# Weight buffers, normalised input tiles and FFN activation tiles begin at eight different 16-byte offsets

## The chip, the core and the metric

The kernel runs on one core of one Trainium2 chip. The metric is the device time of one execution in microseconds (us); lower is better. Before the change the median of three runs is 1369.74 us.

## What is computed

The reference is a decoder trunk of two layers over 512 tokens with a model width of 1024, in float32. Layer 0 is a recurrent mixer (an RG-LRU beside an SSD), layer 1 is dilated attention with 16 heads, and each is followed by a SwiGLU feed-forward network (FFN) with 2816 hidden channels. Cut to its products:

```python
for layer in range(2):
    if layer == 0:
        proj = rmsnorm(x) @ w_in                        # 1024 -> 4624
        ...                                             # convolutions, scans, gates
        x = x + concat(lru_out, ssd_out) @ w_out        # 2048 -> 1024
    else:
        qkv = rmsnorm(x) @ w_qkv                        # 1024 -> 3072
        ...                                             # attention
        x = x + o @ w_out                               # 1024 -> 1024
    g, u = split(rmsnorm(x) @ w_gate_up)                # 1024 -> 2 * 2816
    x = x + (silu(g) * u) @ w_down                      # 2816 -> 1024
```

## The kernel before

Activations lie with channels on the partitions and the 512 tokens along the free axis, so a tile of 128 channels is 128 x 512 float32, 2048 bytes in each partition. A projection of 1024 channels has eight such input tiles.

**Split products.** TensorE multiplies in the format fp32r, which keeps fewer bits than float32. Every operand of a large product is therefore split in two: a high part (the value rounded to fp32r) and a low part (the rest). ScalarE (ACT) writes the high part by a cast, and VectorE (DVE), or GpSimd (POOL) for the attention weights, writes the low part by a subtraction; this is `split` (L82). One product of a weight tile with an input tile is then three matmuls, `mm3` (L104), in a fixed order: low weight with high input (L106), high weight with low input (L107), high with high (L108). Each streams the 512 token columns of the input tile (the moving operand) through 128 x 128 weights that were loaded before (the stationary operand). The load of a matmul's weights (PEld in the profile) runs while the matmul ahead of it streams. In the attention projections (L720 to L722) the roles are turned: the tokens of the input tile are the stationary operand and 512 columns of a weight tile move.

**Weights.** All large weights go through one list of specs in the order of use. `weight(i)` (L89) works two tiles ahead. For tile j it issues one DMA of 128 x 1024 floats into a buffer `wr`, and splits it into `wh` and `wl`. Each of the three has three buffers in turn, of 4096 bytes per partition.

**Inputs.** `Norm.feed` (L179) multiplies a residual tile by the gain of the norm and writes it as `xh` and `xl` into a numbered slot (`slot`, L167); there are twelve slots, and the outputs of the RG-LRU, of the SSD and of the attention heads use the same slots where they fit. The others lie in other pools (`oah`, `oal`, `obh`, `obl`). In the FFN (L645) the silu products are split into `ah` and `al`, twelve buffers of each. A part of 7 or 8 hidden tiles is made by gate and up projections from `xh` and `xl`, and then multiplied by the down weights from `ah` and `al`; there are three such parts in each FFN.

**Counts.** The large products are 5184 matmuls of 512 columns: 2112 gate and up (FFN), 1056 down (FFN), 864 input projections and 384 output projections of the recurrent layer, 576 of q, k and v, and 192 of the attention output.

**Order.** The order on each engine is that in which the code is traced, with waits on semaphores between engines.

**Where the buffers lie.** The program places a buffer at a multiple of 32 bytes in the partition. Taken modulo 512 bytes, every tile of a weight (stationary operand, L106 to L108) starts at byte 96. So do all the slots of `xh` and `xl`; `ah` and `al` start at 288, and `oah`, `oal`, `obh` and `obl` at 480. The small stationary tile `wdt` of L295 starts at 480. The displacement of the moving operand from the stationary one, modulo 512, is thus 0 in 3936 of the 5184 matmuls, 192 in the 1056 of the down projections, and 384 in 192 of the recurrent output projection.

Of the kernel before, what the change touches and what calls it, by code (L numbers as in the profile page):

```python
# [28 lines left out]

# [1 line left out]
_PV = {}  # L31
# [16 lines left out]

# [1 line left out]
_CS = {}  # L50
# [8 lines left out]
def trunk(ctx: ExitStack, tc: tile.TileContext, a):  # L59
# [10 lines left out]

    # ------------------------------------------------------------ weights
    specs = []
# [9 lines left out]
    def split(src, hi, lo, eng=V):  # L82
        S.copy(hi, src)  # L83
        eng.tensor_tensor(out=lo, in0=src, in1=hi.bitcast(F32), op=ALU.subtract)  # L84

    w_of = {}
    emitted = [0]

    def weight(i):  # L89
        while emitted[0] <= min(i + AHEAD, len(specs) - 1):  # L90
            j = emitted[0]
            src, n = specs[j]
            raw = wp.tile([P, WMAX], F32, tag="raw", bufs=NRAW, name=f"wr{j}")
            hi = wp.tile([P, WMAX], F32R, tag="whi", bufs=NSPL, name=f"wh{j}")
            lo = wp.tile([P, WMAX], F32R, tag="wlo", bufs=NSPL, name=f"wl{j}")
            step = n if j else n // 4
            for c in range(0, n, step):
                nc.sync.dma_start(out=raw[:, c:c + step], in_=src[:, c:c + step])
                split(raw[:, c:c + step], hi[:, c:c + step], lo[:, c:c + step], G if src.tensor.name in on_pool else V)
            w_of[j] = (hi, lo)  # L100
            emitted[0] += 1
        return w_of.pop(i, None)
# [6 lines left out]

    # weight order  # L110
    rec_order = [("p", m) for m in (32, 33, 34, 35)]
# [30 lines left out]

    # ------------------------------------------------------------ constants, input
    def load_x(k):
# [12 lines left out]
    def pc(name, i=0, n=1):  # L157
        o, _ = _PV[name]
        return pv[:, o + i:o + i + n]
# [5 lines left out]

    # ------------------------------------------------------------ norm pieces
    def slot(i, dtype):  # L167
        return [xp.tile([P, T], dtype, tag=f"x{z}{i}", name=f"x{z}{i}") for z in "hl"]

# [31 lines left out]
    def rsq_tok(acc, n, eps, tag):  # L201
        """[token, tile] of (sum over partitions of acc / n + eps) ** -0.5"""
        ps = pm.tile([P, T], F32, tag="pm", name="ps_ss")
        for j in range(NT):
            mm(ps[:, j:j + 1], lhsT=acc[:, j * P:(j + 1) * P], rhs=ones[:, 0:1], start=True, stop=True)
        v = sp.tile([P, NT], F32, tag="rv", name="rv")
        V.tensor_scalar(out=v, in0=ps[:, :NT], scalar1=1.0 / n, scalar2=eps, op0=ALU.mult, op1=ALU.add)
        r = sp.tile([P, NT], F32, tag=tag, name=tag)
        G.tensor_tensor(out=r, in0=v, in1=mhalf[:, :NT], op=ALU.pow)
        return r  # L210
# [8 lines left out]

    # work that is traced behind the products of the next projection, which run while its operands are made  # L220
    held = []
# [12 lines left out]

    # ============================================================ layer 0: mixers
    norm = Norm("rec_norm")
# [11 lines left out]
    with ExitStack() as rctx:  # L248
# [6 lines left out]
        rt2 = pctx.enter_context(tc.tile_pool(name="rt2", bufs=2))  # L255
        # dt: the high part of its weights in columns 0..15, the low part in columns 32..47
        wdt = rt2.tile([P, KD, P], F32R, name="wdt", bufs=1)
        G.memset(wdt.rearrange("p k c -> p (k c)").bitcast(mybir.dt.uint32), 0)
        split(wdt_raw, wdt[:, :, :H], wdt[:, :, 32:32 + H])

        # softplus(v) = max(v, 0) + log1p(exp(-|v|)); 1 + u is rounded, and the rest of u is put back
        def softplus(out, v, shape, tag):
# [14 lines left out]

        # --- depthwise causal convolution of a projected tile
        def conv(ps, wname, bname, j, out):
            xin = rp.tile([P, T], F32, tag="cin", name="cin", bufs=2)  # L280
            V.tensor_tensor(out=xin, in0=ps, in1=rb, op=ALU.mult)
            w = lambda t: pc(wname, j * 4 + t)  # noqa: E731
            V.tensor_scalar(out=out, in0=xin, scalar1=w(3), scalar2=pc(bname, j), op0=ALU.mult, op1=ALU.add)
            for t in range(3):
                s = 3 - t
                V.scalar_tensor_tensor(out=out[:, s:], in0=xin[:, :T - s], scalar=w(t), in1=out[:, s:], op0=ALU.mult, op1=ALU.add)

        # --- SSD inputs
        BC = []
# [9 lines left out]
        for j in range(4):  # L299
# [5 lines left out]
            BC.append(t)  # L305
        # --- dt
        dtT = rt2.tile([32 + H, T], F32, name="dtT", bufs=1)
# [14 lines left out]
        softplus(dt, dtv, [P, NH], "sd")  # L322
        # lru: c = -8 softplus(-lambda), halved for the tanh form of the gate
        nlam = rt2.tile([P, 8], F32, name="nlam", bufs=1)
# [65 lines left out]

        # gelu of the gate of tile j
        gg, hs = {}, {}
# [72 lines left out]

        # --- RG-LRU
        lru = {}
# [34 lines left out]

        # --- gated LRU output
        oa = []
# [76 lines left out]

        # --- SSD heads and their gate, with the LRU half of the output projection
        def zlate(j, zz):
# [59 lines left out]

    # ============================================================ feed-forward
    def ffn(norm, idx, after):  # L645
        gu, dn = idx
        with ExitStack() as fctx:
            fp = fctx.enter_context(tc.tile_pool(name="fp", bufs=1))
            pre = [project(gu[0], norm.hl)]
            norm.finish()  # L650
            pre.append(project(gu[KF], norm.hl))
            rb = bcast_tok(norm.rt, fp, "nrb")
            for part, (first, last) in enumerate(HID):
                act = []
                for m in range(first, last):
                    pg, pu = pre if m == 0 else [project(gu[i], norm.hl) for i in (m, m + KF)]
                    tg = fp.tile([P, T], F32, tag="tg", name="tg", bufs=3)
                    tu = fp.tile([P, T], F32, tag="tu", name="tu", bufs=3)
                    V.tensor_tensor(out=tg, in0=pg, in1=rb, op=ALU.mult)  # L659
                    S.activation(tg, tg, AF.Silu)  # L660
                    V.tensor_tensor(out=tu, in0=pu, in1=rb, op=ALU.mult)  # L661
                    V.tensor_tensor(out=tu, in0=tu, in1=tg, op=ALU.mult)
                    hi = fp.tile([P, T], F32R, tag="ah", name="ah", bufs=12)
                    lo = fp.tile([P, T], F32R, tag="al", name="al", bufs=12)
                    split(tu, hi, lo)
                    act.append((hi, lo))
                for m in range(8):
                    ps = project(dn[part, m], act)
                    V.tensor_tensor(out=x[m], in0=ps, in1=x[m], op=ALU.add)  # L669
                    if part == len(HID) - 1:  # L670
                        after(m)
# [3 lines left out]

    # ============================================================ layer 1: attention
    norm = norm2
    norm3 = Norm("ffn_norm1", (8, 9, 10, 11, 4, 5, 6, 7))
    with ExitStack() as actx:
# [6 lines left out]
        gains = []  # L686
        # rotary tables with the gains of the rotated dimensions in them
        tabs = {}
# [16 lines left out]
        def qkv_part(half, w):  # L705
            """projection of 512 columns for all tokens, as a list of steps"""
            pss = []
# [23 lines left out]
        def finish_qk(half, w, t, ps):  # L731
# [10 lines left out]
            V.tensor_tensor(out=q, in0=q, in1=rs.rearrange("p (h o) -> p h o", o=1).to_broadcast([P, 8, 64]), op=ALU.mult)  # L742
            tb = lambda nm: tabs[w, nm][:, t].rearrange("p (o e) -> p o e", o=1).to_broadcast([P, 8, 8])  # noqa: E731
            x1, x2 = q[:, :, 0:8], q[:, :, 8:16]
# [9 lines left out]
        def pair_T(pair):  # L754
            half, p = pair // 4, pair % 4
            for w in range(2):
# [3 lines left out]
                g = gains[w]  # L760
                # head 0 keeps its high part on partitions 0..63, head 1 on partitions 64..127
                hs_ = [ap_.tile([P, T], F32R, tag=f"hi{w}{e}", bufs=2, name="qk_hi") for e in range(2)]
# [19 lines left out]
        oT = []  # L782
        # score rows of token tile i (i + 1 key tiles) and the transposed key tile j (NT - j token tiles), in banks
        S_AT = {3: (0, 0), 0: (1, 0), 2: (1, P), 1: (2, 0)}
# [105 lines left out]

# [1 line left out]
def _tiles(w, kt):  # L892
    """[k, m] -> [m tile, partition of k, k tile, column]"""
    k, m = w.shape
    return w.reshape(kt, P, m // P, P).transpose(2, 1, 0, 3).reshape(m // P, P, kt * P)


def _chan(v):
    """channels -> [partition, tile]"""
    return v.reshape(-1, P).T  # L900
# [6 lines left out]
def _consts():  # L907
# [12 lines left out]
    ang = (np.arange(T, dtype=f)[:, None] * inv[None, :]).astype(f)  # L920
    tok = lambda v: v.reshape(NT, P, 8).transpose(1, 0, 2).reshape(P, NT * 8)  # noqa: E731
    rot = (i % 64) < 16
# [55 lines left out]
```

## Time and profile before

| what | value |
|---|---|
| median of 3 runs | 1369.74 us (1369.41 to 1369.77) |
| profiled execution, first to last instruction (its span) | 1367.8 us |
| profiled execution, time of its own beside the span | not listed; the median of the runs is 1.9 us above the span |
| TensorE busy with matmuls | 1346.5 us, 98% of the span |
| VectorE, ScalarE, GpSimd busy | 797.2, 573.4, 148.5 us |
| mean granted TensorE clock | 0.997 of full speed |

The busy time of TensorE is the union of its matmuls, which overlap: a matmul of 512 columns is recorded with about 390 ns from its start to its modelled end, while the next one starts some 230 ns after it. For the pace of the products the start times are to be compared, and not the durations.

### The profile page before, as it was taken

How to read it: one execution, taken by the hardware profiler on the slowest of the kernel's cores; microseconds unless marked ns; L12 is line 12 of the kernel's file. 1: busy time of each engine (PE TensorE's matmuls, PEld its weight loads, DVE VectorE, ACT ScalarE, POOL GpSimd, SP SyncE). 2: the span in 40 equal slices, each digit the busy share in tenths (PEclk: the TensorE clock that was granted, in tenths of full speed). 3: DMA queues.
4: the chain of work that ended last, by engine and by line, in shares of the span. 5: the costliest groups of instructions: out<-in, count | busy, mean ns of one | idle time of the engine just before them, and what ended most of it. 6: DMA issues, size and time to landing. Idle time of an engine off the chain costs nothing.

```text
span 1367.8 us, 15662 instructions
## 1 busy us (share of the span) xinstructions
PE 1346.5 (98%) x6058; PEld 1081.3 (79%) x6058; DVE 797.2 (58%) x1332; ACT 573.4 (42%) x842; POOL 148.5 (11%) x123
## 2 busy tenths in 40 slices
PE   7999989999999999999999999999999999999998
PEld 6877767888888888888888877777788888888887
DVE  6877799865454334434454777687664434443442
ACT  5743857433332223223333378567642222222321
POOL 0000000000000000000005744554300000000000
PEclk9999999999999999999999999999999999999999
DMA  6322222522233333333232221121033332233332
GB/s 235 109 92 78 93 78 82 165 93 93 92 93 98 103 92 92 92 102 100 85 100 92 77 78 32 62 77 47 18 106 95 105 93 93 91 94 108 93 93 77
DMA packets 38554, 126.50 MB, mean 92 GB/s; under 512 B 4288, under 2 KB 5056, under 8 KB 38352
## 3 DMA queue, kind: packets, MB, share of 16 engines
q1 hardware_dynamic: 38480, 125.51, 29.6%
q8 instruction: 47, 0.77, 0.2%
q14 instruction: 27, 0.22, 0.1%
HBM read 123.36 MB, written 2.13 MB: 92 GB/s over the span
## 4 chain that ended last, share of the span: by engine, by line
PE 87%; DVE 8%; ACT 2%; POOL 2%; issue 1%; DMA 0%; SPq 0%; POOLq 0%; DVEq 0%; ACTq 0%
PE ps_pr L106 24%; PE ps_pr L107 24%; PE ps_pr L108 24%; PE ps_s L803 2%; POOL qrs L741 1%; DVE q L742 1%; PE ps_s L804 1%; PE ps_qkv L721 1%; PE ps_qkv L720 1%; PE ps_qkv L722 1%; PE ps_pT L830 1%; PE ps_o L837 1%; PE ps_ao L106 1%; DVE q L750 1%; PE ps_ao L107 1%; PE ps_yd L543 1%
## 5 line engine op out<-in xcount | busy, mean ns | idle before, releaser
L83 ACT CAST wh<-wr 128x1024 fp32r<-128x1024 f32 (+2 forms) x223 | 228.0, 1023 | 632.7 <-PE ps_pr L108 398.6
L106 PE MATMUL ps_pr<-xh,wl 128*128 128x512 f32 x1056 | 416.9, 395 | 12.2 <-DVE wl L84 11.2
L107 PE MATMUL ps_pr<-xl,wh 128*128 128x512 f32 x1056 | 415.3, 393 | 0.9 <-DVE xl L183 0.9
L108 PE MATMUL ps_pr<-xh,wh 128*128 128x512 f32 x1056 | 414.1, 392 | 0.0
L84 DVE TENSOR_TENSOR wl<-wr,wh 128x1024 fp32r<-128x1024 f32 (+2 forms) x191 | 225.9, 1183 | 52.9 <-ACT wh L83 52.6
L106 PEld LDWEIGHTS ps_pr<-xh,wl 128*128 128x128 f32 x1056 | 199.8, 189 | 55.4 <-DVE wl L84 12.1
L107 PEld LDWEIGHTS ps_pr<-xl,wh 128*128 128x128 f32 x1056 | 199.7, 189 | 43.8 <-DVE xl L183 1.8
L108 PEld LDWEIGHTS ps_pr<-xh,wh 128*128 128x128 f32 x1056 | 199.6, 189 | 42.3 <-issue 0.7
L107 PE MATMUL ps_pr<-al,wh 128*128 128x512 f32 x352 | 138.8, 394 | 0.0
L106 PE MATMUL ps_pr<-ah,wl 128*128 128x512 f32 x352 | 138.8, 394 | 0.0
L108 PE MATMUL ps_pr<-ah,wh 128*128 128x512 f32 x352 | 138.8, 394 | 0.0
L84 POOL TENSOR_TENSOR wl<-wr,wh 128x1024 fp32r<-128x1024 f32 x32 | 78.2, 2448 | 398.7 <-ACT wh L83 398.5
L669 DVE TENSOR_TENSOR x<-ps_pr,x 128x512 f32<-128x512 f32 x48 | 33.2, 692 | 127.7 <-PE ps_pr L108 127.7
L661 DVE TENSOR_TENSOR tu<-ps_pr,nrb 128x512 f32<-128x512 f32 x44 | 30.4, 691 | 130.1 <-PE ps_pr L108 130.1
L659 DVE TENSOR_TENSOR tg<-ps_pr,nrb 128x512 f32<-128x512 f32 x44 | 30.4, 691 | 93.8 <-PE ps_pr L108 93.8
L108 PEld LDWEIGHTS ps_pr<-ah,wh 128*128 128x128 f32 x352 | 65.9, 187 | 16.3
L106 PEld LDWEIGHTS ps_pr<-ah,wl 128*128 128x128 f32 x352 | 65.9, 187 | 16.2
L107 PEld LDWEIGHTS ps_pr<-al,wh 128*128 128x128 f32 x352 | 65.9, 187 | 16.2
L720 PE MATMUL ps_qkv<-wh,xl 128*128 128x512 f32 x192 | 75.6, 394 | 0.5 <-ACT q L734 0.5
L721 PE MATMUL ps_qkv<-wl,xh 128*128 128x512 f32 x192 | 75.7, 394 | 0.0
L722 PE MATMUL ps_qkv<-wh,xh 128*128 128x512 f32 x192 | 75.6, 394 | 0.0
L720 PEld LDWEIGHTS ps_qkv<-wh,xl 128*128 128x128 f32 x192 | 36.1, 188 | 7.8 <-ACT q L734 1.0
(231 smaller groups left out, 1591.3 us busy)
## 6 DMA issues: line engine op xcount, KB each, us to landing
wr<-in_w_gu SPq DMA_DIRECT2D x88, 512.0 KB, 3.5
wr<-in_w_in SPq DMA_DIRECT2D x35, 512.0 KB, 3.6
wr<-in_w_dn SPq DMA_DIRECT2D x32, 448.0 KB, 3.3
wr<-in_w_qkv SPq DMA_DIRECT2D x24, 512.0 KB, 3.5
wr<-in_w_out SPq DMA_DIRECT2D x16, 512.0 KB, 3.5
wr<-in_w_dn SPq DMA_DIRECT2D x16, 512.0 KB, 3.5
x<-in_xT SPq DMA_DIRECT2D x16, 256.0 KB, 3.5
bcs<-csd SPq DMA_DIRECT2D x16, 256.0 KB, 4.1
```

The lines of the kernel that those rows point to most:

```text
L83: S.copy(hi, src)
L84: eng.tensor_tensor(out=lo, in0=src, in1=hi.bitcast(F32), op=ALU.subtract)
L106: mm(ps, lhsT=wl[ws], rhs=xh[xs], start=start, stop=False)
L107: mm(ps, lhsT=wh[ws], rhs=xl[xs], start=False, stop=False)
L108: mm(ps, lhsT=wh[ws], rhs=xh[xs], start=False, stop=stop)
L659: V.tensor_tensor(out=tg, in0=pg, in1=rb, op=ALU.mult)
L661: V.tensor_tensor(out=tu, in0=pu, in1=rb, op=ALU.mult)
L669: V.tensor_tensor(out=x[m], in0=ps, in1=x[m], op=ALU.add)
L720: mm(pss[t], lhsT=xl[:, ts_], rhs=wh[:, cols], start=(k == 0), stop=False)
L721: mm(pss[t], lhsT=xh[:, ts_], rhs=wl[:, cols], start=False, stop=False)
L722: mm(pss[t], lhsT=xh[:, ts_], rhs=wh[:, cols], start=False, stop=(k == KD - 1))
L803: mm(ps, lhsT=q[rows, qs], rhs=kl[rows, :n], start=True, stop=False)
```

## The change

A helper `shifted` allocates a tile with 32 more columns (128 bytes) than wanted and returns the wanted number of columns from an offset of 0, 4, ... or 28 floats, that is 0, 16, ... or 112 bytes. The index that picks the offset is the number of the weight for `wh`, that number divided by 8 for `wl`, the number of the slot for `xh` and of the slot plus 3 for `xl`, and the number of the hidden tile for `ah` and of the tile plus 3 for `al`. The DMA's buffer `wr`, `wdt`, and the tiles `oah`, `oal`, `obh` and `obl` are not shifted, but all that is allocated behind a longer buffer moves with it.

```diff
+    def shifted(pool, n, dtype, i, **kw):
+        o = 4 * (i % 8)
+        return pool.tile([P, n + 32], dtype, **kw)[:, o:o + n]
...
-            hi = wp.tile([P, WMAX], F32R, tag="whi", bufs=NSPL, name=f"wh{j}")
-            lo = wp.tile([P, WMAX], F32R, tag="wlo", bufs=NSPL, name=f"wl{j}")
+            hi = shifted(wp, WMAX, F32R, j, tag="whi", bufs=NSPL, name=f"wh{j}")
+            lo = shifted(wp, WMAX, F32R, j // 8, tag="wlo", bufs=NSPL, name=f"wl{j}")
...
     def slot(i, dtype):
-        return [xp.tile([P, T], dtype, tag=f"x{z}{i}", name=f"x{z}{i}") for z in "hl"]
+        return [shifted(xp, T, dtype, i + 3 * (z == "l"), tag=f"x{z}{i}", name=f"x{z}{i}") for z in "hl"]
...
-                    hi = fp.tile([P, T], F32R, tag="ah", name="ah", bufs=12)
-                    lo = fp.tile([P, T], F32R, tag="al", name="al", bufs=12)
+                    hi = shifted(fp, T, F32R, m, tag="ah", name="ah", bufs=12)
+                    lo = shifted(fp, T, F32R, m + 3, tag="al", name="al", bufs=12)
```

The rest of the difference is comments taken out. Every engine keeps its instructions, their order and their waits; only addresses differ. In the built program the displacement of the moving from the stationary operand takes all 32 multiples of 16 bytes modulo 512, each in 136 to 184 of the 5184 matmuls.

## Rows read from the trace of the kernel before

**Rows 1.** The page: busy time by engine, slices of TensorE and its clock.

```profile
PE 1346.5 (98%) x6058; PEld 1081.3 (79%) x6058; DVE 797.2 (58%) x1332; ACT 573.4 (42%) x842; POOL 148.5 (11%) x123
...
PE   7999989999999999999999999999999999999998
...
PEclk9999999999999999999999999999999999999999
```

**Rows 2.** The page: the chain that ended last, shares of the span by engine.

```profile
PE 87%; DVE 8%; ACT 2%; POOL 2%; issue 1%; DMA 0%; SPq 0%; POOLq 0%; DVEq 0%; ACTq 0%
```

**Rows 3.** Waits: who waited for whom, us, times, longest.

```profile
ACT wh L83 <- PE ps_pr L108: 398.6, 119, 8.9
...
PE ps_pr L106 <- DVE wl L84: 11.2, 3, 6.0
```

**Rows 4.** Timeline of TensorE, FFN gate and up: start, duration; first to last 176 intervals.

```profile
400.03 0.39 PE L108 MATMUL ps_pr<-xh,wh 128*128 128x512 f32 x1
400.26 0.39 PE L106 MATMUL ps_pr<-xh,wl 128*128 128x512 f32 x1
...
439.93 0.39 PE L107 MATMUL ps_pr<-xl,wh 128*128 128x512 f32 x1
```

**Rows 5.** Timeline of TensorE, FFN down; 111 intervals from the first to the last.

```profile
575.06 0.40 PE L106 MATMUL ps_pr<-ah,wl 128*128 128x512 f32 x1
575.29 0.39 PE L107 MATMUL ps_pr<-al,wh 128*128 128x512 f32 x1
...
600.96 0.40 PE L106 MATMUL ps_pr<-ah,wl 128*128 128x512 f32 x1
```

**Rows 6.** Busy time and counts in a gate-and-up and a down stretch: us, PE, PEld, DVE, ACT, POOL.

```profile
400.00:460.00 60.00, 60.00 (x265) 49.44 (x264) 27.10 (x32) 17.33 (x21) 0.00 (x0) 1.00 0.33 98
575.00:600.00 25.00, 25.00 (x108) 20.04 (x108) 8.92 (x10) 4.70 (x5) 0.00 (x0) 1.00 0.33 99
```

**Rows 7.** Timeline of TensorE, recurrent output projection, tiles ob; first to last 12 intervals.

```profile
331.22 0.39 PE L106 MATMUL ps_pr<-obh,wl 128*128 128x512 f32 x1
...
331.68 0.40 PE L108 MATMUL ps_pr<-obh,wh 128*128 128x512 f32 x1
331.92 0.39 PE L106 MATMUL ps_pr<-obh,wl 128*128 128x512 f32 x1
332.14 0.40 PE L107 MATMUL ps_pr<-obl,wh 128*128 128x512 f32 x1
332.38 0.39 PE L108 MATMUL ps_pr<-obh,wh 128*128 128x512 f32 x1
...
334.01 0.39 PE L106 MATMUL ps_pr<-xh,wl 128*128 128x512 f32 x1
```

**Rows 8.** The chain in order of time: start, us, what; two longer pieces.

```profile
16.56 3.72 PE ps_dt L295 x16
...
88.70 2.58 PE ps_st L432 x6
```

**Rows 9.** Timeline, start of the second FFN; from 1006.74 first 11, then 7 intervals.

```profile
1005.61 0.95 PE L205 MATMUL ps_ss<-cst,nacc 128*128 128x1 f32 x8
1006.42 0.48 PE L107 MATMUL ps_pr<-xl,wh 128*128 128x512 f32 x1
1006.74 0.39 PE L108 MATMUL ps_pr<-xh,wh 128*128 128x512 f32 x1
1006.97 0.40 PE L106 MATMUL ps_pr<-xh,wl 128*128 128x512 f32 x1
...
1009.27 0.39 PE L107 MATMUL ps_pr<-xl,wh 128*128 128x512 f32 x1
...
1010.86 0.39 PE L108 MATMUL ps_pr<-xh,wh 128*128 128x512 f32 x1
```

**Rows 10.** Groups by shape: convolution steps, and splits; busy us, mean ns, idle before.

```profile
L286 DVE SCALAR_TENSOR_TENSOR cv<-cin,pv,cv 128x509 f32<-128x509 f32 x12 | 8.9, 745 | 0.2
L286 DVE SCALAR_TENSOR_TENSOR cv<-cin,pv,cv 128x511 f32<-128x511 f32 x12 | 8.8, 744 | 0.1
...
L549 DVE SCALAR_TENSOR_TENSOR xs<-xs,pv,ps_yd 128x512 f32<-128x512 f32 x8 | 6.0, 746 | 6.1 <-PE ps_yd L543 6.1
```

**Rows 11.** The page: groups of the casts and subtractions of the weights.

```profile
L83 ACT CAST wh<-wr 128x1024 fp32r<-128x1024 f32 (+2 forms) x223 | 228.0, 1023 | 632.7 <-PE ps_pr L108 398.6
...
L84 DVE TENSOR_TENSOR wl<-wr,wh 128x1024 fp32r<-128x1024 f32 (+2 forms) x191 | 225.9, 1183 | 52.9 <-ACT wh L83 52.6
...
L84 POOL TENSOR_TENSOR wl<-wr,wh 128x1024 fp32r<-128x1024 f32 x32 | 78.2, 2448 | 398.7 <-ACT wh L83 398.5
```

## Prediction

> **What bounds the kernel now.** I read the page first. TensorE is busy in 98% of the span, in nearly all of its slices nine tenths or more, and its granted clock is full throughout [rows 1]. The chain that ended last runs through TensorE for 87% of the span; VectorE has 8%, ACT and POOL 2% each, DMA none [rows 2]. So the pace of the matmuls sets the time. The waits agree: the longest is ACT's, 398.6 us, for the matmul that frees a weight buffer, while the matmuls wait 11.2 us in all for their split weights [rows 3]. The weights are early, TensorE is late.
>
> Next comes the pace itself, read from start times. In the gate and up projections of the FFN the reader sees a start every 0.22 or 0.23 us: 39.90 us for 176 intervals, 226.7 ns each [rows 4]. In the down projections it is 25.90 us for 111 intervals, 233.3 ns [rows 5]. Both are matmuls of 512 columns with 128 x 128 weights, at the full clock of 2.4 GHz, without a gap: busy time equals the length of both stretches [rows 6]. At one column per cycle 512 columns take 213.3 ns. Each matmul so pays 13.4 or 20.0 ns beyond its columns, and the 5184 together some 80 us. The two stages don't differ in instruction, clock or waits. They differ in addresses: the moving operand lies 0 bytes (modulo 512) from the stationary one in gate and up, 192 bytes in down.
>
> Two more places show a dependence. Where `ob` moves, at displacement 384, starts alternate between some 0.23 and 0.24 us, 2.79 us for 12 intervals, 232.5 ns [rows 7]. The 16 products with `wdt`, 128 bytes off, take 3.72 us, 232.5 ns each [rows 8]. Displacement 0 alone doesn't give the short pace either: behind an interruption at the start of the second FFN the same operands take 2.53 us for 11 intervals, 230.0 ns, and only then 1.59 us for 7, 227.1 ns [rows 9]. So 226.7 ns looks like a steady state into which a run of matmuls settles when one matmul stands to the next always in the same way.
>
> **The change, part by part.** No instruction, byte of DMA or wait is added or taken away. What can change is how fast an engine passes through its operands.
>
> *VectorE, ACT and POOL* read or write shifted tiles. The convolution steps already write and read at starts 4 to 12 bytes off the tile: 509 and 511 elements take 745 and 744 ns, and the same kind of instruction on an unshifted tile of 512 takes 746 [rows 10]. I take nothing for these engines. The bound: the splits of the weights take 228.0 + 225.9 + 78.2 = 532 us [rows 11]; one per cent of that is 5 us, which ACT's 398.6 us of waiting for TensorE cover [rows 3], and which would be added to the time if the weights were no longer early.
>
> *The load of the weights* lies under the matmul ahead of it, 49.4 us of loads in 60 us and 20.0 us in 25 us [rows 6]. It costs nothing as long as it stays shorter than the matmul; that a load slows the running matmul is part of the next term.
>
> *The matmuls.* After the change the displacement differs from one matmul to the next in 96% of the cases, and takes all 32 values about equally. Which pace does that give? The trace shows four values other than the settled one: 233.3 (displacement 192), 232.5 (384), 232.5 (128) and 230.0 (0, not settled) [rows 5, 7 to 9]. Their mean is 232.1 ns. Displacement 0 now holds in 155 of the 5184 matmuls, and in two running in 8 places, so I expect the settled state nowhere, and take 232 ns for all. That is an estimate from these rows: no row shows a displacement that isn't a multiple of 64 bytes. The sum, for each kind of product:
>
> - gate and up, 2112 x (232.0 - 226.7) = +11.2 us;
> - down, 1056 x (232.0 - 233.3) = -1.4 us;
> - the 192 with `oa` and `ob` outside the slots, 192 x (232.0 - 232.5) = -0.1 us;
> - the other 1824 (input projections, half of the recurrent output, q, k, v, attention output), where interruptions are frequent: between settled and not, (226.7 + 230.0) / 2 = 228.4 ns, so 1824 x 3.6 = +6.6 us.
>
> That is +16.3 us. The chain outside TensorE is 13% of the span [rows 2], mostly in the attention, where a slower matmul may be hidden; but a share of the last term alone is at stake, some 1 us, and I leave it in. The profiled span of 1367.8 us becomes 1384.1 us, and with the 1.9 us between span and median the forecast is **1386 us**, 1.2% slower. The pace of all 5184 matmuls moves the time by 5.2 us per ns; that one number carries the forecast.
>
> *Its bounds.* The least that the products could need: six passes of 512 columns in plain fp32 (L432) take 2.58 us, 430.0 ns each, 3.3 ns more than two cycles per column, so a matmul may cost only some 3.3 ns beyond its columns [rows 8]. At 216.6 ns everywhere the gains are 21.3 + 17.6 + 3.1 + 21.5 = 64 us, and the time 1306 us. The most: the longer of the alternating intervals, 240 ns [rows 7], everywhere: +28.1 + 7.1 + 1.4 + 21.2 = +58 us, 1428 us. I stay near the middle, because every pair of operands with another displacement came out within 1 ns of 232.5 on average.
>
> **The skill beside it.** The Trainium skill, page "TensorE: Matmul & The Clock Gate", Part 2, says that TensorE has two independent read ports into SBUF, so that loading the next weights takes no bandwidth from the running matmul; its back-to-back gap is N / 2.4 + 2.5, 215.7 ns measured for 512 columns. By that rule addresses would not matter and the time would stay. The trace doesn't agree on either: 226.7 and 233.3 ns at the same clock [rows 4, 5]. That is the third rival's case, since what differs might yet be something other than the displacement.
>
> **The rivals.**
>
> *Faster: the even spacing is what collides.* Before, all displacements are multiples of 64 bytes. If the 13 to 20 ns come from both streams meeting in the same part of the memory, then offsets of 16 bytes could make them miss each other in part of the matmuls. It decides from a mean below 228.9 ns, where the sum above is nil: (2112 x 226.7 + 1056 x 233.3 + 192 x 232.5 + 1824 x 228.4) / 5184. With half of all matmuls at 216.6 ns and half at 232 the mean is 224.3 and the time 1369.7 - 4.6 x 5.2 = 1346 us. For it speaks that no row shows such an offset. Against it: it must hold on average over all 32 displacements, and the three values other than 0 that the trace has are all slower than the settled 0.
>
> *Much slower: no steady state at all.* Each matmul meets the one ahead at a new displacement; if each then pays the long interval of the alternation without the short one that follows, the mean goes towards 236 ns, halfway from 232 to 240, and the time to 1386 + 4 x 5.2 = 1407 us. Against it: in [rows 7] a long interval is followed by a short one, so the loss isn't paid twice.
>
> *No change: it isn't the displacement.* All operands with a longer pace (`ah`, `al`, `ob`, `wdt`) also lie in other pools, behind the weights in the partition, and the fast pairs ahead of them. If that place, and not the offset, sets the pace, then the shifts of up to some kilobytes change nothing: 1369.7 us. Against it: `ob` alternates while `ah` and `al` are even, at neighbouring places, and displacement 0 has two paces at one place [rows 5, 7, 9].
>
> **How the numbers follow.** A run before differs from another by some tenths of a us; 0.2%, 2.7 us, is about what a measurement can tell from no change, and corresponds to 0.5 ns of pace. Chances: the forecast case, slower with a pace from 229.5 to 235 ns, 1373 to 1402 us, 0.60; much slower, above that, 0.06; no change 0.13; faster 0.21. The forecast case alone has the range 1373 to 1402. For 8 times in 10 I take in no change and the near part of the faster case: **1358 to 1402 us**, which leaves out 0.06 above and some 0.13 below. Faster 0.21, same 0.13, slower 0.66.
>
> **What would show it.** In the changed kernel's timeline, the gate and up projections should lose their even 226.7 ns and show intervals that wander between some 224 and 240 ns with a mean near 232; the down projections should wander as well, with a mean little below 233.3. Splits on ACT and VectorE should keep their durations within a per cent and TensorE its full clock. The prediction is wrong if gate and up stay even at 226.7 (no change), or if their mean falls below that (faster): then some displacements that the trace of before doesn't hold are better than 0, and the intervals, sorted by displacement, would show which.

## The result and the profile after

The changed kernel takes 1380.76 us (1380.38 to 1381.49, four runs), the kernel before on the same chip 1369.58 us; the ratio is 1.0086, with a 95% interval from 1.0074 to 1.0098. It is slower by 11.2 us. The forecast was 1386 us, so it was 5 us too high and inside its range. The mean granted clock differs a little from run to run: beside the later experiments the kernel before took 1369.4 us where it was 0.997 and 1368.0 us where it was 0.999 (medians of seven and six runs). All four runs of the changed kernel have 0.999, so at equal clock the change costs rather 12 us, an estimate from these figures.

The page of the changed kernel: busy time by engine, the clock, and the chain that ended last (they answer to [rows 1] and [rows 2]).

```profile
span 1379.1 us, 15662 instructions
...
PE 1360.4 (99%) x6058; PEld 1082.0 (78%) x6058; DVE 797.3 (58%) x1332; ACT 573.5 (42%) x842; POOL 148.7 (11%) x123
...
PEclk9999999999999999999999999999999999999999
...
PE 94%; DVE 4%; ACT 1%; issue 0%; DMA 0%; SPq 0%; POOL 0%; DVEq 0%; ACTq 0%
```

The span grew by 11.3 us and the busy time of TensorE by 13.9 us, at a mean clock of 0.999 for 0.997, while the other engines are as busy as before. More of the chain lies in TensorE, 94% for 87%, and the parts of VectorE and GpSimd in it shrank: where the products became slower, waits beside them were covered.

The timeline of TensorE in the changed kernel, gate and up (columns as in [rows 4]); 167 intervals from the first to the last row.

```profile
401.25 0.39 PE L113 MATMUL ps_pr<-xh,wh 128*128 128x512 f32 x1
401.48 0.40 PE L111 MATMUL ps_pr<-xh,wl 128*128 128x512 f32 x1
...
402.40 0.40 PE L112 MATMUL ps_pr<-xl,wh 128*128 128x512 f32 x1
402.64 0.40 PE L113 MATMUL ps_pr<-xh,wh 128*128 128x512 f32 x1
402.88 0.39 PE L111 MATMUL ps_pr<-xh,wl 128*128 128x512 f32 x1
403.10 0.39 PE L112 MATMUL ps_pr<-xl,wh 128*128 128x512 f32 x1
...
439.93 0.39 PE L112 MATMUL ps_pr<-xl,wh 128*128 128x512 f32 x1
```

The even step of 0.22 or 0.23 us is gone: starts follow after 0.22, 0.23 or 0.24 us, and the mean is 38.68 / 167 = 231.6 ns where it was 226.7 [rows 4].

The same in the down projections, 111 intervals, beside [rows 5].

```profile
580.16 0.40 PE L111 MATMUL ps_pr<-ah,wl 128*128 128x512 f32 x1
...
605.91 0.39 PE L111 MATMUL ps_pr<-ah,wl 128*128 128x512 f32 x1
```

That is 25.75 / 111 = 232.0 ns, a little below the 233.3 of before. All start times of the trace, taken together with the addresses of the built program, give a mean of 231.7 ns for some 5000 large matmuls. Sorted by displacement, the 32 means lie between 231.0 and 232.5 ns; at displacement 0, which settled at 226.7 ns before, it is 231.4 ns. So it isn't that some of the new displacements are bad and others good: in this sequence all cost nearly the same.

Groups of the splits of the weights in the changed kernel, beside [rows 11].

```profile
L83 ACT CAST wh<-wr 128x1024 fp32r<-128x1024 f32 (+2 forms) x223 | 227.6, 1021 | 645.3 <-PE ps_pr L113 404.5
...
L84 DVE TENSOR_TENSOR wl<-wr,wh 128x1024 fp32r<-128x1024 f32 (+2 forms) x191 | 225.8, 1183 | 52.7 <-ACT wh L83 52.4
```

The casts and subtractions onto shifted tiles take what they took before, 227.6 us for 228.0 and 225.8 us for 225.9.

Where the time went, by stage: windows over the recurrent layer, the first FFN, the attention and the second FFN (us, then busy time of PE, PEld, DVE, ACT and POOL). First the kernel before:

```profile
6.00:361.40 355.40, 348.71 (x1601) 277.16 (x1602) 276.91 (x456) 195.89 (x257) 3.04 (x3) 0.99 0.35 111
361.40:726.10 364.70, 364.70 (x1602) 299.00 (x1601) 165.33 (x194) 106.12 (x130) 6.87 (x3) 1.00 0.31 94
726.10:997.90 271.80, 267.94 (x1257) 206.36 (x1256) 194.93 (x488) 170.97 (x334) 135.48 (x111) 1.00 0.20 62
997.90:1363.50 365.60, 364.74 (x1602) 298.73 (x1600) 157.77 (x188) 97.88 (x118) 1.94 (x1) 1.00 0.31 95
```

and the same four stages of the changed kernel:

```profile
6.20:363.20 357.00, 351.63 (x1601) 276.89 (x1602) 276.84 (x456) 195.20 (x255) 3.04 (x3) 1.00 0.34 109
363.20:732.40 369.20, 369.20 (x1602) 299.58 (x1601) 165.36 (x194) 106.07 (x130) 6.88 (x3) 1.00 0.31 93
732.40:1005.40 273.00, 270.17 (x1257) 206.31 (x1256) 195.28 (x488) 171.37 (x335) 135.67 (x111) 1.00 0.20 62
1005.40:1374.80 369.40, 368.94 (x1601) 299.21 (x1600) 157.45 (x188) 97.63 (x117) 1.94 (x1) 1.00 0.31 94
```

The two FFNs lost 4.5 and 3.8 us, the recurrent layer 1.6 and the attention 1.2. In the recurrent layer TensorE was busy 2.9 us longer and idle 1.3 us less (6.7 to 5.4 us), in the attention 2.2 us longer and idle 1.0 us less (3.9 to 2.8).

A part of the recurrent layer's figure is the clock. TensorE waits there some 4 us for a low weight tile and then runs for a while at a lower granted clock, in both kernels. The same stretch before and after (the last three numbers are the clock, the DMA share and GB/s):

```profile
180.00:190.00 10.00, 6.93 (x19) 5.49 (x20) 10.00 (x16) 1.22 (x2) 0.00 (x0) 0.66 0.16 52
180.00:190.00 10.00, 6.23 (x21) 4.65 (x20) 10.00 (x15) 2.27 (x3) 0.00 (x0) 0.83 0.17 52
```

Behind that wait 11 matmuls of the kernel before start 427 ns apart, at the level of 1.2 GHz, and 7 of the changed kernel: four fewer, 200 ns each, 0.8 us in favour of the changed kernel's profile.

### The profile page after: what moved, and what is told of

It reads as the page before. It is cut to its first block, busy times and chain, and to the rows that moved or that the text cites. A ratio compares the mean times of both kernels' runs of the same rounds, so it can differ in the third digit from the quotient of the medians.

```text
span 1379.1 us, 15662 instructions
## 1 busy us (share of the span) xinstructions
PE 1360.4 (99%) x6058; PEld 1082.0 (78%) x6058; DVE 797.3 (58%) x1332; ACT 573.5 (42%) x842; POOL 148.7 (11%) x123
## 4 chain that ended last, share of the span: by engine, by line
PE 94%; DVE 4%; ACT 1%; issue 0%; DMA 0%; SPq 0%; POOL 0%; DVEq 0%; ACTq 0%
PE ps_pr L111 24%; PE ps_pr L112 24%; PE ps_pr L113 24%; PE ps_qkv L725 3%; PE ps_qkv L726 3%; PE ps_qkv L727 3%; PE ps_s L808 1%; PE ps_s L809 1%; PE ps_pT L835 1%; PE ps_o L842 1%; PE ps_ao L111 1%; PE ps_yd L548 1%; PE ps_ao L112 1%; PE ps_ao L113 1%; PE ps_o L843 1%; PE ps_qT L764 1%
## 5 line engine op out<-in xcount | busy, mean ns | idle before, releaser
L83 ACT CAST wh<-wr 128x1024 fp32r<-128x1024 f32 (+2 forms) x223 | 227.6, 1021 | 645.3 <-PE ps_pr L113 404.5
L111 PE MATMUL ps_pr<-xh,wl 128*128 128x512 f32 x1056 | 420.6, 398 | 11.2 <-DVE wl L84 10.6
L84 DVE TENSOR_TENSOR wl<-wr,wh 128x1024 fp32r<-128x1024 f32 (+2 forms) x191 | 225.8, 1183 | 52.7 <-ACT wh L83 52.4
L111 PEld LDWEIGHTS ps_pr<-xh,wl 128*128 128x128 f32 x1056 | 199.6, 189 | 58.8 <-DVE wl L84 11.4
L726 PEld LDWEIGHTS ps_qkv<-wl,xh 128*128 128x128 f32 x192 | 36.1, 188 | 7.8 <-issue 0.2
```

Of the source, the lines that this page charges most:

```text
L111: mm(ps, lhsT=wl[ws], rhs=xh[xs], start=start, stop=False)
L726: mm(pss[t], lhsT=xh[:, ts_], rhs=wl[:, cols], start=False, stop=False)
```

## The experiments

The theory to test: what sets the pace is how the two operands lie to each other, and the short pace needs the same displacement in matmul after matmul. Its rivals: each shifted operand costs by itself; every displacement but 0 is slow by itself; the 16-byte offsets cost and the length doesn't; the place of a buffer in the partition counts; the place of an operand's start within a block of memory counts.

### Each half of the change alone

Weights shifted as in the change, inputs and activations allocated as before (the FFN activations lie 768 bytes further on, behind the longer buffers; the inputs don't move):

```diff
+            hi = shifted(wp, WMAX, F32R, j, tag="whi", bufs=NSPL, name=f"wh{j}")
+            lo = shifted(wp, WMAX, F32R, j // 8, tag="wlo", bufs=NSPL, name=f"wl{j}")
```

> Only the weight buffers are shifted and longer, inputs and FFN activations stay as before. Theory: a run of matmuls settles to 226.7 or 233.3 ns only while the displacement of the moving from the stationary operand stays the same from one matmul to the next; where it varies the pace wanders, whatever the displacements are. Within one weight the low and the high tile now lie at different displacements, so gate and up wander near 231.7 ns and the time is that of the whole change, 1378 to 1382 us. Rival (the start of the moving operand in its own line of memory counts): the moving operands lie as before, so 226.7 ns and 1369.6 us.

Measured: 1382.09 us, ratio 1.0099 (1.0082 to 1.0116). The timeline of this kernel, gate and up, 169 intervals:

```profile
401.69 0.39 PE L111 MATMUL ps_pr<-xl,wh 128*128 128x512 f32 x1
...
440.95 0.39 PE L112 MATMUL ps_pr<-xh,wh 128*128 128x512 f32 x1
```

39.26 / 169 = 232.3 ns. The moving operands of gate and up lay at the addresses where they had lain before, so their own starts aren't the cause.

The other half, input slots and FFN activations shifted, weights as before:

```diff
+        return [shifted(xp, T, dtype, i + 3 * (z == "l"), tag=f"x{z}{i}", name=f"x{z}{i}") for z in "hl"]
...
+                    hi = shifted(fp, T, F32R, m, tag="ah", name="ah", bufs=12)
+                    lo = shifted(fp, T, F32R, m + 3, tag="al", name="al", bufs=12)
```

> Only the input slots and the FFN activations are shifted and longer, the weights stay as before. Theory: the displacement varies again from matmul to matmul, so a pace near 231.7 ns in gate, up and down, and 1377 to 1382 us: each part alone costs nearly what both cost together. Rival (each shifted operand costs by itself): the costs of this run and of the run with shifted weights add up to the 11.2 us of the change, some 5 to 6 us here.

Measured: 1380.30 us, ratio 1.0084 (1.0069 to 1.0099). The timeline, gate and up, 171 intervals:

```profile
401.74 0.39 PE L112 MATMUL ps_pr<-xh,wh 128*128 128x512 f32 x1
...
441.35 0.39 PE L112 MATMUL ps_pr<-xh,wh 128*128 128x512 f32 x1
```

39.61 / 171 = 231.6 ns, which is also the mean over all large matmuls. Each half alone costs about what both cost together: 13.2 and 11.4 us beside the 11.2 us of the change. The costs don't add up, so it isn't a price per shifted operand.

### Which displacement settles at which pace

High and low weight tiles get one offset that holds for three weights and then grows by 16 bytes; the buffers are 512 bytes longer, so that all three of a kind lie alike:

```diff
+            o = 4 * ((j // 3) % 32)
+            hi = wp.tile([P, WMAX + 128], F32R, tag="whi", bufs=NSPL, name=f"wh{j}")[:, o:o + WMAX]
+            lo = wp.tile([P, WMAX + 128], F32R, tag="wlo", bufs=NSPL, name=f"wl{j}")[:, o:o + WMAX]
```

> High and low weight tiles get one common offset that stays for three weights (72 matmuls) and then grows by 16 bytes, through all 32 values. Theory: after a few matmuls each step settles to an even pace of its own; 226.7 ns at displacement 0, 233.3 at 192, an alternation with a mean of 232.5 at 384; the others may lie anywhere from 216 to 240, and a mean over all steps near 231. Rival (any displacement but 0 is slow by itself): one even pace of 232 to 233 ns in all steps but 0. Rival (the place of a buffer in the partition counts): 226.7 ns in all steps of gate and up, 233.3 in all of down.

Measured (one run, 1381.54 us): from the start times of each step, without the ten intervals behind its start and behind each interruption, and with both halves of 512 bytes taken together, since they agree (steps with fewer than ten intervals left are not counted):

| displacement modulo 256, bytes | settled pace, ns |
|---|---|
| 0 | 226.7 |
| 16 | 226.7, in one step of 24 matmuls |
| 240 | 226.7 in three steps, 233.3 in one |
| 64 | 228.9 in five steps, 233.3 in one |
| 80 | 230.0 |
| 176 | 231.1 to 232.1 |
| 128 | 232.4 to 233.1 |
| 32, 48, 96, 112, 144, 192, 208, 224 | 233.3 (from 231.6 to 233.5) |
| 160 | 234.3 |

Two steps at displacement 64 from the timeline of this kernel, the first with 52 intervals and the second with 51:

```profile
545.67 0.40 PE L108 MATMUL ps_pr<-xl,wh 128*128 128x512 f32 x1
...
557.80 0.40 PE L109 MATMUL ps_pr<-xh,wh 128*128 128x512 f32 x1
...
1167.78 0.39 PE L109 MATMUL ps_pr<-xh,wh 128*128 128x512 f32 x1
...
1179.46 0.39 PE L109 MATMUL ps_pr<-xh,wh 128*128 128x512 f32 x1
```

12.13 / 52 = 233.3 ns and 11.68 / 51 = 229.0 ns for the same operands: a displacement can have two settled paces. So it is at displacement 240, in two steps of 23 and 71 intervals:

```profile
362.52 0.40 PE L107 MATMUL ps_pr<-xh,wl 128*128 128x512 f32 x1
...
367.89 0.39 PE L109 MATMUL ps_pr<-xh,wh 128*128 128x512 f32 x1
...
620.90 0.39 PE L107 MATMUL ps_pr<-xh,wl 128*128 128x512 f32 x1
...
637.00 0.40 PE L109 MATMUL ps_pr<-xh,wh 128*128 128x512 f32 x1
```

5.37 / 23 = 233.5 ns and 16.10 / 71 = 226.8 ns. What decides between the two was not found. Place in the partition can't explain steps within one buffer. Some displacements other than 0 are short too, so "any but 0 is slow" falls as it was put, but most of them are. No displacement is better than 0. The plain mean over the 16 values is 231.8 ns, close to the changed kernel's 231.7; that this mean is the reason for it is not shown.

### The FFN activations brought to displacement 0

One unused tile of 320 bytes ahead of the activations, nothing else:

```diff
+            pad = fp.tile([P, 80], F32, name="pad")
+            V.memset(pad, 0.0)
             pre = [project(gu[0], norm.hl)]
```

> The kernel before with one unused tile of 320 bytes ahead of the FFN activations, so that they start at byte 96 modulo 512 as the weights do. Theory: down settles at 226.7 ns instead of 233.3, 1056 x 6.7 ns = 7.0 us, so 1362.5 us. Rival (the place of a buffer in the partition counts): the activations stay where they were but for 320 bytes, down stays at 233.3 ns and the time at 1369.6 us.

Measured: 1361.75 us, ratio 0.9949 (0.9934 to 0.9964). The timeline of this kernel, down projections, 110 intervals:

```profile
571.93 0.39 PE L106 MATMUL ps_pr<-ah,wl 128*128 128x512 f32 x1
...
596.87 0.39 PE L108 MATMUL ps_pr<-ah,wh 128*128 128x512 f32 x1
```

24.94 / 110 = 226.7 ns, where 233.3 stood [rows 5]. That is 1056 x 6.6 ns = 7.0 us, and 7.1 us were measured. The activations lie at the same place but for 320 bytes, so it isn't their place behind the weights that made them slow.

### All operands at displacement 0

The run before with 128 bytes of padding more, in the recurrent layer:

```diff
+        hpad = hp.tile([P, 32], F32, name="hpad")
+        V.memset(hpad, 0.0)
         sctx = ExitStack()
```

> The FFN activations aligned as in the run before, and 128 bytes of padding more, so that the other tiles of the recurrent layer's outputs and the small tile of the dt weights start at byte 96 modulo 512 too: all 5184 matmuls have displacement 0. Theory: 192 more matmuls go from 232.5 to 226.7 ns, 1.1 us, so 1360.7 us and a ratio of 0.994 to the kernel before. Rival (the place of these tiles counts): no more than the aligned FFN activations gave, 1361.8 us.

Measured: 1360.77 us, ratio 0.9944 (0.9932 to 0.9957): some 8 us faster than the kernel before. The 192 matmuls go from 232.7 to 226.7 ns in the trace. The last microsecond is as large as expected, but the interval doesn't separate it from the run with the aligned activations. The page of this kernel:

```profile
span 1357.1 us, 15666 instructions
...
PE 1336.0 (98%) x6058; PEld 1080.1 (80%) x6058; DVE 797.2 (59%) x1335; ACT 574.0 (42%) x842; POOL 148.8 (11%) x123
```

TensorE is busy 10.5 us less than in [rows 1], with the same matmuls; 0.8 us of that is the clock again (7 matmuls at 427 ns for 11).

### The longer buffers without the offsets

```diff
-        o = 4 * (i % 8)
+        o = 0
```

> The changed kernel with every offset set to 0: the buffers are 128 bytes longer and nothing else, so that neighbouring buffers lie at different multiples of 128 bytes modulo 512 and the displacement varies in multiples of 64. Theory: varying displacement is what costs, so the length alone brings the pace to some 231.7 ns and the time to 1378 to 1382 us. Rival (the 16-byte offsets cost, the length doesn't): 1369 us.

Measured: 1383.95 us, ratio 1.0113 (1.0100 to 1.0127), a little dearer than the whole change with 1.0086 (1.0074 to 1.0098). The timeline, gate and up, 168 intervals:

```profile
401.83 0.40 PE L113 MATMUL ps_pr<-xh,wh 128*128 128x512 f32 x1
...
440.87 0.39 PE L113 MATMUL ps_pr<-xh,wh 128*128 128x512 f32 x1
```

39.04 / 168 = 232.4 ns. The 128 bytes alone are enough to take neighbouring buffers out of step.

This kernel also says something on which weights count. Sorted by the displacement modulo 256 from a matmul's own weights, the intervals of its large matmuls have means of 232.7 ns at 0, 231.4 at 128 and 233.1 to 233.3 at 64 and 192. Sorted by the displacement from the weights of the next matmul, which load while this one streams, they have 230.7 ns at 0 and 233.0 to 233.4 at the others. Where only its own weights lie at 0 the mean is 232.9 ns, where only the next ones do it is 230.0. That points to the load that runs under the stream. It isn't settled: with one displacement for all matmuls the two are the same, and no run was made to part them.

### A variation by 256 bytes, and one by 16

Only the weights are shifted, by 0 or 256 bytes:

```diff
+            oh, ol = 64 * (j % 2), 64 * (j // 8 % 2)
+            hi = wp.tile([P, WMAX + 128], F32R, tag="whi", bufs=NSPL, name=f"wh{j}")[:, oh:oh + WMAX]
+            lo = wp.tile([P, WMAX + 128], F32R, tag="wlo", bufs=NSPL, name=f"wl{j}")[:, ol:ol + WMAX]
```

> Only the weights are shifted, by 0 or 256 bytes, differently for high and low tiles. In the staircase the settled paces repeat after 256 bytes (64 and 320, 80 and 336, 160 and 416). Theory: only the displacement modulo 256 counts, so gate and up stay at 226.7 ns and the time at 1369 us. Rival (any variation from one matmul to the next breaks the settled run): a pace near 231.7 ns where high and low tiles differ, in half of the weights, and 1375 us or more.

Measured: 1368.65 us, ratio 1.0001 (0.9992 to 1.0010), no change. The timeline, gate and up, 172 intervals:

```profile
401.82 0.39 PE L107 MATMUL ps_pr<-xh,wl 128*128 128x512 f32 x1
...
440.81 0.39 PE L108 MATMUL ps_pr<-xl,wh 128*128 128x512 f32 x1
```

38.99 / 172 = 226.7 ns. Displacements that differ by 256 are alike, and a variation between them costs nothing.

The smallest variation: only the low tiles are shifted, always by 16 bytes.

```diff
+            lo = wp.tile([P, WMAX + 128], F32R, tag="wlo", bufs=NSPL, name=f"wl{j}")[:, 4:4 + WMAX]
```

> Only the low weight tiles are shifted, by 16 bytes, always the same: displacements in gate and up go -16, 0, 0 and so on. Both settle at 226.7 ns in the staircase when held. Theory A (the pace belongs to the displacement): 226.7 ns and 1369 us. Theory B (a change from one matmul to the next is what unsettles the run, however small): a pace of 229 to 232 ns in gate and up, and 1375 to 1381 us.

Measured: 1377.52 us, ratio 1.0067 (1.0052 to 1.0082). The timeline, gate and up, 169 intervals:

```profile
401.71 0.39 PE L108 MATMUL ps_pr<-xh,wh 128*128 128x512 f32 x1
...
440.96 0.40 PE L106 MATMUL ps_pr<-xh,wl 128*128 128x512 f32 x1
```

39.25 / 169 = 232.2 ns. Held, displacement 0 settles at 226.7 ns, and -16 (240 modulo 256) at 226.7 in three steps and 233.3 in one. Even with 233.3 for it the mean of the three would be 228.9 ns; in turn they cost 232.2. So the pace isn't a property of each displacement: the step from one matmul to the next counts. It can also help: in down the same kernel has 176, 192, 192. 111 intervals there:

```profile
576.88 0.40 PE L106 MATMUL ps_pr<-ah,wl 128*128 128x512 f32 x1
...
602.30 0.39 PE L106 MATMUL ps_pr<-ah,wl 128*128 128x512 f32 x1
```

25.42 / 111 = 229.0 ns, less than either displacement has when held (232.0 and 233.3).

### All operands moved together

All displacements 0 and 416 bytes of padding ahead of everything, so that all operands start at byte 0 modulo 512:

```diff
+    cpad = cp.tile([P, 104], F32, name="cpad")
+    V.memset(cpad, 0.0)
     cst = cp.tile([P, NCS], F32, name="cst")
```

> As the run with all displacements 0, but 416 bytes of padding ahead of all other buffers, so that every operand of the 5184 matmuls starts at byte 0 modulo 512 and no longer at 96 (which is 32 modulo 64). Theory: only the displacement between the two operands counts, not where each starts; 226.7 ns and 1360.8 us, ratio 0.994, as before the move. Rival (an operand that starts within a 64-byte block costs one block more per matmul, which is the same in all kernels so far): a pace of 224 ns or less in gate and up, 1347 us or less.

Measured: 1361.33 us, ratio 0.9942 (0.9928 to 0.9955). The timeline, gate and up, 174 intervals:

```profile
395.78 0.39 PE L106 MATMUL ps_pr<-xh,wl 128*128 128x512 f32 x1
...
435.22 0.39 PE L106 MATMUL ps_pr<-xh,wl 128*128 128x512 f32 x1
```

39.44 / 174 = 226.7 ns. Between these two places, byte 96 and byte 0, it doesn't matter where both operands start, as long as they lie alike.

## Why the prediction was right, and where it was off

**The bound.** Right: TensorE's pace set the time, and every kernel above follows it.

**The engines that write the shifted tiles.** Right: nothing, as the splits' 227.6 and 225.8 us show. The loads of the weights stayed below the matmuls.

**The pace of 232 ns.** Right: 231.7 ns in the mean, 231.6 in gate and up, 232.0 in down, which gained a little, as forecast. The estimate was made from four rows of which none had an offset of 16 bytes. That the mean of those four, 232.1 ns, came so near was in part luck: the table of the staircase has short values too (226.7 at 0 and 16, 228.9 to 230.0 at 64 and 80), but only some five of its 16, and no row of before held one other than 0. The 230.0 ns of displacement 0, one of the four, is a mean over a start that was still settling, not a pace that was held [rows 9]. That the settled state is lost is shown by displacement 0 itself, 226.7 ns before and 231.4 ns in the changed kernel, and by the run with -16, 0, 0. "Wander" was too loose a word: in several runs the intervals repeat after three or more matmuls, in step with the displacements; the state is another one rather than none.

**The sum of 16.3 us.** The direction and mechanism were right, sizes were off: 11.3 us were measured in the span. Set side by side matmul for matmul, the two profiles give for gate and up +9.7 us where +11.2 was forecast (226.8 to 231.5 ns, half a ns short of 232.0), for down -1.5 where -1.4 was forecast, and -0.1 for the 192 as forecast. The step that failed most is the cover of the last term, "the other 1824", with +6.6 us: the recurrent layer and the attention gave 1.6 + 1.2 = 2.8 us. The price of their products was right: where they stand back to back in both profiles they became slower by 3.7 + 2.6 = 6.3 us in all. But more than half of that didn't reach the time. Some 0.8 us is the clock, four fewer matmuls at 427 ns in the recurrent layer. Most of the rest went into TensorE's own idle time (2.3 us less), since VectorE's and GpSimd's work ran on as before and had been what TensorE waited for. The prediction put that cover at some 1 us and left it in the sum.

**The rivals.** *No change, by the place in the partition:* refuted by the aligned activations, 226.7 ns at the same place but for 320 bytes. The Trainium skill, page "TensorE: Matmul & The Clock Gate", Part 2, has the load of the next weights on a read port of its own that takes nothing from the running matmul. The runs here don't fit a load that takes nothing whatever the addresses: 226.7 or 233.3 ns by the displacement alone. That it is the load which slows the stream is not shown. *Faster, by offsets of 16 bytes:* no displacement of the staircase is below 226.7 ns. *Much slower:* no stage came near 236 ns.

**What stays open.** That a displacement counts modulo 256, whichever operand is moved, points to the two reads meeting in the memory; how they meet was not measured, nor whether the weights that count are the matmul's own or those of the next, nor why one displacement can settle at two paces. The best settled pace is still 10 ns above the 216.6 ns that were worked out from the fp32 passes as a bound, and nothing here says whether the rest can be had.

## What to carry to other kernels

Read the pace of matmuls from start to start and compare it between stages that should be equal: 226.7 against 233.3 ns was the clue here, and the recorded durations, 0.39 or 0.40 us in both stages, don't show it. Where fp32r products run back to back as in this kernel, try operands that all start alike modulo 256 bytes; 320 bytes of padding ahead of a pool gave 0.5% here. Making buffers 128 bytes longer or spreading their starts changes these displacements, also for what lies behind them, and cost 1.1% and 0.9%; 512 bytes more with starts apart by 256 cost nothing (1.0001).

## What was not expected of the hardware

The pace depends on the displacement modulo 256 bytes, with short values at 0, +16 and mostly -16 (226.7 ns) and at 64 and 80 (229 to 230 ns), and 231 to 234 ns at the others. The same displacement can settle at two paces (233.3 and 229.0 ns at 64), so something besides it counts, perhaps what ran before. And a repeated change of 16 bytes between low and high tiles costs 5.5 ns per matmul in gate and up, although both displacements can run at 226.7 ns when held.
